# Attention outputs stored undivided, row sums inverted through DRAM

## The chip, the core and the metric

The kernel runs on one NeuronCore of a Trainium2 chip. TensorE (PE in the rows) multiplies matrices into PSUM, VectorE (DVE), ScalarE (ACT) and GpSimd (POOL) work on elements, and SyncE (SP) mostly issues DMAs; each of them takes its instructions strictly in order. The metric is the device time of one execution in microseconds (us). Two runs of the same kernel agree to a fraction of a per cent.

## The reference

A two-layer transformer backbone on 1024 latent and 256 context tokens of width 1024. Layer 0 mixes tokens by eight heads of latent attention (and, beside them, four heads of gated linear attention); layer 1 uses a gated delta rule; each layer ends in a squared-ReLU MLP. The change touches the attention heads of layer 0 and what reads their output:

```python
s = jnp.einsum('bhqd,bhkd->bhqk', qblk, k).astype(F32) * scale
p = jax.nn.softmax(s, axis=-1).astype(v.dtype)
return jnp.einsum('bhqk,bhkv->bhqv', p, v)
...
return jnp.concatenate([att, gla.reshape(B, L, GLA_HEADS * GLA_DV)], axis=-1) @ w_out
```

The softmax divides each query's exponentials by their sum, so an output may be accumulated undivided and divided later, by one number per head and query.

## The kernel before

Features lie on the partitions and tokens along the free dimension, in three blocks (`BLOCKS`): tokens 0 to 511, 512 to 1023, and the 256 context tokens. Every matrix product is made of three passes of reduced precision: each operand is split into a leading part (`...h`, `hi`, made by an ACT copy) and a rest (`...l`, `lo`, made by a subtraction on POOL or DVE), and PE adds hi·hi, hi·lo and lo·hi (lines 181 to 183).

**Attention** goes over heads 0 to 7, within a head over the three query blocks, and within a block over ten tiles of 128 keys (two for the context block): 176 steps. A step computes transposed scores `S` (three matmuls), takes their exponential `P` on ACT (L907), splits it into `ph` (ACT or DVE, L911 and L913) and `pl` (POOL, in one step of four DVE, L914), and four steps later multiplies it with the values (`pv`, lines 873 to 875). The value tile `Vh` carries 64 columns of ones, so PSUM tile `acc` holds 64 rows of outputs and 64 equal rows of the sums of the exponentials. At the last key tile of a block, 24 times in all, DVE inverts the 64 rows of sums (L878), multiplies (L880), and SP stores the result into `d_mix` in DRAM (L882). Beside this, `max_ops` finds the row maxima of the next blocks' scores (PE matmuls `M` L855, DVE reductions `mx` L856 and `mr` L858, PE `pr` L862), and `pair_ops` projects keys and queries of the next two heads.

**Output projection** (`out_proj`): `prep0(k, b)` loads chunk k of 128 features (two heads for k below 4) of block b from `d_mix` into `mx_in` (L806) and splits it. Block 0 is prepared while heads 6 and 7 still run; pass 0 multiplies it with the eight column blocks m of the weights, and meanwhile the 16 chunks of blocks 1 and 2 are prepared for pass 1. DVE also adds each result to the residual (`h`, L969) and adds up products for a modulation (`acc`, L124 and L126, fed by `adaw` DMAs on SP's queue); at the end of pass 0 PE sums squares (`st`, L252).

The Python code is a sequence of emissions. The build may place an instruction ahead of others that it doesn't depend on, so the order on an engine is read from the built program.

Of the kernel before, what the change touches and what calls it, by code (L numbers as in the profile page):

```python
# [33 lines left out]
def hybrid_backbone(ctx: ExitStack, tc: tile.TileContext, a, out, taps=None):  # L34
# [25 lines left out]
    def pump(us):  # L60
        """advances every lane: a lane yields the vector engine's time of what it emitted, or None to wait for the next call."""
        for it in list(lanes):
            gen, w = it
            t = us * w
            while t > 0:
                try:
                    d = next(gen)
                except StopIteration:
                    lanes.remove(it)
                    break  # L70
                if d is None:
                    break
                t -= d
# [39 lines left out]
    def ada_lane(l, mods, cols, wpool, accpool, ppool, ptag, wait=1):  # L113
        """modulations of layer l: products on the vector engine, sums over the partitions on the tensor engine."""
# [25 lines left out]
    def ada_first(m, half, wpool, ypool, ppool):  # L140
        """half of a modulation of layer 0 before there is other work: products on the tensor engine, then transposed."""
# [43 lines left out]
    def group(ps, n, nk, w, x, rate, every=1e9):  # L185
        """ps = sum over k of w(k)^T x(k), split operands; the lanes advance by rate of its time."""
# [12 lines left out]
    def rsqrt_small(p, ssq, n, dim, gain=1.0):  # L199
        """ssq: AP [128, n] (sums); returns tile [128, n] with gain/sqrt(mean + eps): a seed from the exponent, a step of  # L200
        third and one of second order."""
# [16 lines left out]
    def rsqrt_pool(p, ssq, n, dim):  # L218
        """as rsqrt_small, on the pool engine."""
# [13 lines left out]
    def stat_lane(hs, c0, n, tp, small, pp, ptag, dim, inc=False, engs=(V, G)):  # L233
        """1/rms of the tokens c0..c0+n over the features in the tiles hs, [128 tokens, n/128]; inc: as the tiles are made."""
# [22 lines left out]
    def spread(r, nt, pp, ptag):  # L257
        """r [128 tokens, nt] along the free dimension, the same on every partition: PSUM [128, nt * 128]."""
# [10 lines left out]
    def norm_lane(hs, c0, n, A, B, dst, tp, small, pp, ptag, r=None, inc=False, rb=None, ks=range(KD)):  # L269
        """a = rms(h) * A + B of a block of tokens, split into dst(k)."""  # L270
# [21 lines left out]
    class Act:  # L292
        """split activations [features, tokens] in tiles of one block of tokens."""
# [13 lines left out]
    # =========================================================== layer 0 mixer  # L307
# [8 lines left out]
    d_mix = [dram.tile([128, T], F32, name=f"d_mix{i}") for i in range(KD)]  # L316

# [13 lines left out]
    def gla_gates(g):  # L331
        """per head: decays of both directions (partitions 0..63 forward, 64..127 backward), decayed queries and keys."""
# [62 lines left out]
    def gla_main(g):  # L395
        """per head: states before every chunk, outputs, norm over the head, gate; transposed into d_mix."""
        f_order = list(range(16, 20)) + list(range(16))
        b_order = list(range(19, 15, -1)) + list(range(15, -1, -1))
        for h in range(4):
# [4 lines left out]
            # a chunk's outer product goes to the slot of the state after it  # L404
# [109 lines left out]
    with ExitStack() as e1:  # L514
# [146 lines left out]
        def latent(j, i, hs):  # L661
            """a chunk of the query (j = 0) or key-value (j = 1) latents, with its part of the sums of squares."""
# [26 lines left out]
    # ---- multi-head latent attention: scores transposed, minus the queries' maxima in a row of the contraction  # L689
# [7 lines left out]
    def proj(m, nm, kt, xh, xl, w, pp, tag):  # L697
        """generator of the projected blocks."""
# [8 lines left out]
    with ExitStack() as e2:  # L707
# [26 lines left out]
        # values  # L734
# [12 lines left out]
        # rotated query parts, scaled  # L747
# [46 lines left out]
    lp, wm = [None], [None]  # L794
# [7 lines left out]
    def prep0(k, b, eng):  # L802
        """a chunk of the heads' outputs, split for the output projection."""
        c0, n = BLOCKS[b]
        x = lp[0].tile([128, 512], F32, name="mx_in")
        nc.sync.dma_start(out=x[:, :n], in_=d_mix[k][:, c0:c0 + n])  # L806
        split(x[:, :n], *mix.at(k, c0, n), eng)

    with ExitStack() as e2:
# [8 lines left out]
        def pair_ops(m):  # L818
            """projections of the heads 2m, 2m + 1 into their slots, a block of tokens at a time."""
# [24 lines left out]
        def max_ops(hd, b):  # L844
            """the row maxima of the scores of a block of queries into the contraction's last row: subtracted as rounded to
            the leading part, which the softmax does not depend on."""
# [19 lines left out]
        def pv(st):  # L866
# [9 lines left out]
            if last:  # L876
                rt = op_.tile([64, 512], F32, name="rt")
                V.reciprocal(out=rt[:, :n], in_=o[64:128, :n])  # L878
                ot = op_.tile([64, 512], F32, name="ot")
                V.tensor_tensor(out=ot[:, :n], in0=o[0:64, :n], in1=rt[:, :n], op=ALU.mult)  # L880
                r0 = 64 * (hd % 2)
                nc.sync.dma_start(out=d_mix[hd // 2][r0:r0 + 64, c0:c0 + n], in_=ot[:, :n])  # L882

        acc = [None]
        steps = []
# [11 lines left out]
        for hd, b, j, last in steps:  # L897
# [27 lines left out]
            if (hd, b, j) == (7, 1, 9):  # L925
# [7 lines left out]
        for st in pend:  # L933
            pv(st)
    ea.close()
    elp.close()

    # =========================================================== output projection, residual; MLP
# [7 lines left out]
    def out_proj(l, wname, passes, mix, prep, base, act, add, stack, wp, w, span, sp=None):  # L946
        """h = base + gate * (mix @ w) in passes over blocks of tokens; prep[b]: what makes the blocks of pass b."""
# [42 lines left out]
    def mlp(l, blocks, tail_blocks, act, lanes_in, tail, wp, then=None):  # L990
        """h += gate * mlp(act); lanes_in(pools) makes the blocks after the first, tail(pools, b) follows a finished block."""
# [70 lines left out]
    with ExitStack() as e1:  # L1062
        mp = pool(e1, "mixT")
        mix.add(mp, "mx", BLOCKS[1:2])
        lp[0] = pool(e1, "lo", 3)
# [31 lines left out]
    # =========================================================== layer 1 mixer: gated delta rule  # L1097
# [720 lines left out]
```

## Time and profile before

| | us |
|---|---|
| timed runs | 3552.53, 3552.6, 3554.66 |
| median | 3552.6 |
| profiled execution: span from first to last instruction | 3550.4 |
| TensorE busy | 3322.8 (94%) |
| VectorE busy | 2329.7 (66%) |
| attention stage, from 575 to 933 us of the span | 358 |

No other time of the profiled execution is given than its span; it stands 2.2 us below the median of the timed runs, and that is taken for what lies around the span. In the rows below a busy TensorE isn't one at its peak, since matmuls overlap; how many matmuls start in a stretch tells more. "[2.60 <-DVE ot L880]" behind a row says that the engine was idle for 2.60 us before it, until that instruction ended. SPq is SP's queue of DMA issues. PEclk is the granted clock of TensorE as a share of 2.4 GHz.

### The profile page before, as it was taken

The page shows a single profiled execution, that of the slowest core. Times are in us where ns is not written, and L with a number is a line of the kernel's source. Part 1 is how long each engine was busy: PE and PEld are TensorE (multiplying, and loading weights), DVE is VectorE, ACT ScalarE, POOL GpSimd, SP SyncE. Part 2 cuts the span into 40 slices and gives each one's busy share as a digit, 9 for nine tenths or more (in the row PEclk, how much of TensorE's full clock was granted, in tenths as well). Part 3 has the DMA queues.
Part 4 walks back from the last instruction along what each step waited for, and adds up shares of the span by engine and source line. Part 5 has one row for each costly group of instructions (what it writes and reads, how often), then busy time and mean ns, then how long its engine had stood idle before and what let it go on. Part 6 is the DMA issues. An engine that isn't in the chain of part 4 may idle for free.

```text
span 3550.4 us, 47773 instructions
## 1 busy us (share of the span) xinstructions
PE 3322.8 (94%) x18372; PEld 2736.7 (77%) x18372; DVE 2329.7 (66%) x3986; ACT 1156.1 (33%) x2153; POOL 1077.5 (30%) x809
## 2 busy tenths in 40 slices
PE   8998988999989999999999997877999999999998
PEld 4876766666778888888888776666888788888887
DVE  4847556888768777776445779998466554444445
ACT  3143336555423111111211453332465421111212
POOL 3212125556642111111211332334025522222223
PEclk9988889999989999999999999998999999999999
DMA  5622224101422222221111233333664211111111
GB/s 191 216 71 64 59 92 105 26 21 50 149 88 84 75 82 80 76 82 62 45 39 36 72 101 90 90 83 103 143 131 131 72 48 48 48 48 48 48 54 60
DMA packets 279155, 285.06 MB, mean 80 GB/s; under 512 B 152176, under 2 KB 217264, under 8 KB 278928
## 3 DMA queue, kind: packets, MB, share of 16 engines
q1 hardware_dynamic: 267120, 260.78, 25.3%
q0 software_dynamic: 5760, 10.75, 1.3%
q10 hardware_dynamic: 6048, 10.49, 0.9%
q8 instruction: 144, 2.36, 0.3%
q14 instruction: 83, 0.68, 0.1%
HBM read 228.67 MB, written 53.28 MB: 79 GB/s over the span
## 4 chain that ended last, share of the span: by engine, by line
PE 71%; DVE 17%; issue 4%; ACT 3%; DMA 3%; POOL 2%; SPq 0%; DVEq 0%; ACTq 0%; POOLq 0%
PE ps L181 17%; PE ps L183 17%; PE ps L182 17%; DVE acc L126 2%; DVE tm L1371 2%; DVE gst L445 1%; DMA adaw<-in_adaw_dram 1%; DVE X L1373 1%; PE S L181 1%; DVE y L1151 1%; PE S L183 1%; PE S L182 1%; PE pa L1620 1%; DVE X L1365 1%; PE M L855 1%
## 5 line engine op out<-in xcount | busy, mean ns | idle before, releaser
L170 POOL TENSOR_TENSOR wlo<-wst,whi 128x1024 fp32r<-128x1024 f32 (+1 forms) x207 | 488.6, 2368 | 1553.1 <-ACT whi L167 1528.4
L181 PE MATMUL ps<-th,whi 128*128 128x512 f32 (+1 forms) x1304 | 480.5, 368 | 4.9 <-DVE h L1045 3.4
L183 PE MATMUL ps<-th,wlo 128*128 128x512 f32 (+1 forms) x1304 | 477.4, 366 | 2.4 <-POOL wlo L170 2.4
L167 ACT CAST whi<-wst 128x1024 fp32r<-128x1024 f32 (+2 forms) x213 | 212.6, 1012 | 820.1 <-PE ps L182 740.1
L182 PE MATMUL ps<-tl,whi 128*128 128x512 f32 (+1 forms) x1304 | 478.4, 367 | 0.0
L1010 DVE TENSOR_TENSOR rl<-rl 128x512 f32<-128x512 f32 (+1 forms) x160 | 214.5, 1341 | 346.0 <-ACT rl L1009 345.8
L181 PE MATMUL ps<-mxh,whi 128*128 128x512 f32 (+1 forms) x1008 | 356.5, 354 | 0.0
L183 PE MATMUL ps<-mxh,wlo 128*128 128x512 f32 (+1 forms) x1008 | 351.1, 349 | 1.1 <-POOL wlo L170 1.1
L182 PE MATMUL ps<-mxl,whi 128*128 128x512 f32 (+1 forms) x1008 | 351.5, 349 | 0.0
L126 DVE SCALAR_TENSOR_TENSOR acc<-adaw,sc,acc 128x256 f32<-128x256 f32 (+1 forms) x476 | 293.8, 661 | 42.5 <-DMA adaw<-in_adaw_dram 42.0
L1045 DVE SCALAR_TENSOR_TENSOR h<-ps,mod,h 128x512 f32<-128x512 f32 (+1 forms) x384 | 243.8, 657 | 96.4 <-PE ps L183 94.7
L181 PEld LDWEIGHTS ps<-th,whi 128*128 128x128 f32 x1304 | 247.4, 190 | 48.7 <-DVE h L1045 4.7
L183 PEld LDWEIGHTS ps<-th,wlo 128*128 128x128 f32 x1304 | 247.0, 189 | 43.6 <-POOL wlo L170 3.2
L182 PEld LDWEIGHTS ps<-tl,whi 128*128 128x128 f32 x1304 | 247.6, 190 | 38.9
L1045 DVE SCALAR_TENSOR_TENSOR g<-ps,mod,g 128x512 f32<-128x512 f32 (+1 forms) x264 | 188.5, 731 | 106.3 <-PE ps L183 106.1
L914 POOL TENSOR_TENSOR pl<-P,ph 128x512 fp32r<-128x512 f32 x144 | 179.7, 1262 | 114.3 <-DVE ph L913 78.9
L181 PEld LDWEIGHTS ps<-mxh,whi 128*128 128x128 f32 x1008 | 194.4, 193 | 25.8 <-issue 1.2
L182 PEld LDWEIGHTS ps<-mxl,whi 128*128 128x128 f32 x1008 | 194.4, 193 | 24.9 <-issue 1.4
L183 PEld LDWEIGHTS ps<-mxh,wlo 128*128 128x128 f32 x1008 | 194.2, 193 | 25.0 <-POOL wlo L170 1.5
L183 PE MATMUL ps<-m1h,wlo 128*128 128x512 f32 x512 | 203.9, 398 | 0.0
L181 PE MATMUL ps<-m1h,whi 128*128 128x512 f32 x512 | 203.8, 398 | 0.0
L182 PE MATMUL ps<-m1l,whi 128*128 128x512 f32 x512 | 203.6, 398 | 0.0
(373 smaller groups left out, 7011.6 us busy)
## 6 DMA issues: line engine op xcount, KB each, us to landing
wst<-in_w_dram SPq DMA_DIRECT2D x128, 512.0 KB, 3.5
adaw<-in_adaw_dram SPq DMA_DIRECT2D x224, 128.0 KB, 2.1
adaw<-in_adaw_dram SPq DMA_DIRECT2D x80, 256.0 KB, 3.6
wst<-in_owT_dram SPq DMA_DIRECT2D x25, 512.0 KB, 3.8
wst<-in_ewo_dram SPq DMA_DIRECT2D x16, 512.0 KB, 3.7
wY<-d_YA SPq DMA_DIRECT2D x64, 128.0 KB, 3.2
wst<-in_owo_dram SPq DMA_DIRECT2D x16, 512.0 KB, 3.7
wst<-in_ewT_dram SPq DMA_DIRECT2D x14, 512.0 KB, 4.6
```

The source lines that it names most:

```text
L126: V.scalar_tensor_tensor(out=acc[c], in0=w, scalar=sc[:, k, c:c + 1], in1=acc[c], op0=ALU.mult, op1=ALU.add)
L167: S.copy(out=hi, in_=src)
L170: lo_eng.tensor_tensor(out=lo, in0=src, in1=hi.bitcast(F32), op=ALU.subtract)
L181: PE.matmul(ps, hi_w, hi_x, start=first, stop=False)
L182: PE.matmul(ps, hi_w, lo_x, start=False, stop=False)
L183: PE.matmul(ps, lo_w, hi_x, start=False, stop=last)
L445: V.scalar_tensor_tensor(out=stt[p0:p0 + 64, c2, :], in0=stt[p0:p0 + 64, c, :], scalar=ge[p0:p0 + 64, c:c + 1], in1=stt[p0:p0 + 64, c2, :] ...
L855: PE.matmul(ps[:, :kn_], qh[0:96, qt * 128:(qt + 1) * 128], kh[0:96, k0:k0 + kn_], start=True, stop=True)
L914: (V if j % 4 == 3 else G).tensor_tensor(out=pl[:, :n], in0=P_[:, :n], in1=ph[:, :n].bitcast(F32), op=ALU.subtract)
L1010: V.tensor_tensor(out=r[:, :n], in0=r[:, :n], in1=r[:, :n], op=ALU.mult)
L1045: V.scalar_tensor_tensor(out=h[m][:, c0:c0 + n], in0=ps[:, :n], scalar=mod[l][:, 40 + m, c:c + 1], in1=h[m][:, c0:c0 + n], op0=ALU.mult, o ...
L1371: V.tensor_tensor(out=t3, in0=X[:, k + 1:, k:k + 1].to_broadcast([128, n, k]), in1=X[:, k:k + 1, :k].to_broadcast([128, n, k]), op=ALU.mult)
```

## The change

The division leaves the attention stage. At the last key tile ACT copies 65 rows of `acc` (64 of outputs, one of sums) into SBUF; SP stores the sums into `d_sum` and the undivided outputs into `d_mix`. After both heads of a pair have stored a block, `rcp_ops` loads their sums as 128 partitions by 8 (or 4) numbers, inverts these on DVE three steps later, and stores them into `d_rcp`. `prep0` loads the inverses for k below 4, each row repeated over 64 partitions, and DVE multiplies (`mx_r`, new line 813). In pass 1 the pool has two `mx_in` buffers and one `mx_r` where it had three `mx_in`. `prep0(3, 0)` is emitted later, at the last step. The rest of the diff takes out comments.

```diff
+    d_sum = dram.tile([8, T], F32, name="d_sum")
+    d_rcp = dram.tile([8, T], F32, name="d_rcp")
...
-    lp, wm = [None], [None]
+    lp, wm = [None, 2], [None]
...
         x = lp[0].tile([128, 512], F32, name="mx_in")
         nc.sync.dma_start(out=x[:, :n], in_=d_mix[k][:, c0:c0 + n])
+        if k < 4:
+            r = lp[0].tile([128, 512], F32, name="mx_r", bufs=lp[1])
+            for i in range(2):
+                nc.sync.dma_start(out=r[64 * i:64 * i + 64, :n], in_=d_rcp[2 * k + i, c0:c0 + n].partition_broadcast(64))
+            V.tensor_tensor(out=x[:, :n], in0=x[:, :n], in1=r[:, :n], op=ALU.mult)
         split(x[:, :n], *mix.at(k, c0, n), eng)
...
             if last:
-                rt = op_.tile([64, 512], F32, name="rt")
-                V.reciprocal(out=rt[:, :n], in_=o[64:128, :n])
-                ot = op_.tile([64, 512], F32, name="ot")
-                V.tensor_tensor(out=ot[:, :n], in0=o[0:64, :n], in1=rt[:, :n], op=ALU.mult)
+
+                ot = op_.tile([65, 512], F32, name="ot")
+                S.copy(out=ot[:, :n], in_=o[0:65, :n])
                 r0 = 64 * (hd % 2)
-                nc.sync.dma_start(out=d_mix[hd // 2][r0:r0 + 64, c0:c0 + n], in_=ot[:, :n])
+                nc.sync.dma_start(out=d_sum[hd:hd + 1, c0:c0 + n], in_=ot[64:65, :n])
+                nc.sync.dma_start(out=d_mix[hd // 2][r0:r0 + 64, c0:c0 + n], in_=ot[0:64, :n])
+                if hd % 2:
+                    rcps.append(rcp_ops(hd // 2, c0, n))
+
+        def rcp_ops(m, c0, n):
+
+            w = n // 64
+            sm = small.tile([128, 8], F32, name="sm")
+            for i in range(2):
+                nc.sync.dma_start(out=sm[64 * i:64 * i + 64, :w], in_=d_sum[2 * m + i, c0:c0 + n].rearrange("(q w) -> q w", w=w))
+            for _ in range(3):
+                yield
+            sq = small.tile([128, 8], F32, name="sq")
+            V.reciprocal(out=sq[:, :w], in_=sm[:, :w])
+            for i in range(2):
+                nc.sync.dma_start(out=d_rcp[2 * m + i, c0:c0 + n].rearrange("(q w) -> q w", w=w), in_=sq[64 * i:64 * i + 64, :w])
...
-            if (hd, b, j) == (7, 1, 9):
+            for x in list(rcps):
+                if next(x, 1):
+                    rcps.remove(x)
+            if (hd, b, j) == (7, 2, NT - 1):
                 prep0(3, 0, G)
...
+        for x in rcps:
+            run(x)
...
-        lp[0] = pool(e1, "lo", 3)
+        lp[:] = pool(e1, "lo", 2), 1
```

In the built program, first place: VectorE at the end of head 1 and the start of head 2. Before, from the inversion of block 1 of head 1 on:

```order
L878 RECIPROCAL rt<-acc 64x512
L913 CAST ph<-P 128x512
L880 TENSOR_TENSOR ot<-acc,rt 64x512
L856 TENSOR_REDUCE mx<-M 128x1 x2
L914 TENSOR_TENSOR pl<-P,ph 128x512
L856 TENSOR_REDUCE mx<-M 128x1 x2
L878 RECIPROCAL rt<-acc 64x256
```

Now, the same stretch, with the inversions of both heads' sums, blocks 1 and 2 (old L914, L856 and L913 are L937, L863 and L936):

```order
L937 TENSOR_TENSOR pl<-P,ph 128x512
L863 TENSOR_REDUCE mx<-M 128x1 x2
L936 CAST ph<-P 128x512
L902 RECIPROCAL sq<-sm 128x8
L863 TENSOR_REDUCE mx<-M 128x1 x2
L865 TENSOR_REDUCE mr<-mx 128x4
L936 CAST ph<-P 128x512
L902 RECIPROCAL sq<-sm 128x4
```

The long inversions and the products behind them have left the place; two inversions of 8 and 4 numbers per partition stand some rows later.

Second place: VectorE where attention ends and the projection begins. Before (`h_7919` is the first residual sum of pass 0):

```order
L878 RECIPROCAL rt<-acc 64x512
L878 RECIPROCAL rt<-acc 64x256
L880 TENSOR_TENSOR ot<-acc,rt 64x512
L880 TENSOR_TENSOR ot<-acc,rt 64x256
L124 TENSOR_SCALAR acc_8023<-adaw,sc 128x256
L124 TENSOR_SCALAR acc_8024<-adaw,sc 128x256
L126 SCALAR_TENSOR_TENSOR acc_8023<-adaw,sc,acc_8023 128x256
L126 SCALAR_TENSOR_TENSOR acc_8024<-adaw,sc,acc_8024 128x256
L969 SCALAR_TENSOR_TENSOR h_7919<-ps,mod_79,h_7919 128x512
```

Now (`h_7997` is that sum, line 813 the product for chunk 3 of block 0):

```order
L813 TENSOR_TENSOR mx_in<-mx_in,mx_r 128x512
L902 RECIPROCAL sq<-sm 128x8
L124 TENSOR_SCALAR acc_8101<-adaw,sc 128x256
L124 TENSOR_SCALAR acc_8102<-adaw,sc 128x256
L126 SCALAR_TENSOR_TENSOR acc_8101<-adaw,sc,acc_8101 128x256
L126 SCALAR_TENSOR_TENSOR acc_8102<-adaw,sc,acc_8102 128x256
L902 RECIPROCAL sq<-sm 128x4
L997 SCALAR_TENSOR_TENSOR h_7997<-ps,mod_79,h_7997 128x512
```

Ahead of the first residual sum VectorE now has a product and two inversions that depend on DMAs, where it had 6 us of its own work.

Third place: SP's queue there. Before, from the last store of an output to the first weights of the projection behind it:

```order
L882 DMA d_mix_104<-ot 64x256
L121 DMA adaw<-in_adaw_dram 128x256 x2
L806 DMA mx_in<-d_mix_104 128x512
L806 DMA mx_in<-d_mix_105 128x512
L121 DMA adaw<-in_adaw_dram 128x256
L806 DMA mx_in<-d_mix_106 128x512
L121 DMA adaw<-in_adaw_dram 128x256
L174 DMA wst<-in_ewo_dram 128x1024
```

Now, behind the same store:

```order
L898 DMA sm<-d_sum 64x8
L121 DMA adaw<-in_adaw_dram 128x256 x2
L898 DMA sm<-d_sum 64x4
L808 DMA mx_in<-d_mix_101 128x512
L904 DMA d_rcp<-sq 64x8 x2
L121 DMA adaw<-in_adaw_dram 128x256
L904 DMA d_rcp<-sq 64x4 x2
L121 DMA adaw<-in_adaw_dram 128x256
L812 DMA mx_r<-d_rcp 64x512 x2
L121 DMA adaw<-in_adaw_dram 128x256
L808 DMA mx_in<-d_mix_102 128x512
L121 DMA adaw<-in_adaw_dram 128x256
```

The loads of sums, the stores of inverses and the loads of `mx_r`, each of which waits for the one before, now stand among the loads for pass 1, with the `adaw` loads and the next weights behind them.

## Rows read from the trace of the kernel before

**Rows 1.** The page: its span, and TensorE's busy time over the span.
```profile
span 3550.4 us, 47773 instructions
PE 3322.8 (94%) x18372; PEld 2736.7 (77%) x18372; DVE 2329.7 (66%) x3986; ACT 1156.1 (33%) x2153; POOL 1077.5 (30%) x809
```
**Rows 2.** Windows: us; PE, PEld, DVE, ACT, POOL busy (count); PEclk, DMA, GB/s.
```profile
575.00:933.00 358.00, 331.71 (x1464) 251.95 (x1463) 292.82 (x420) 193.91 (x345) 223.92 (x194) 0.96 0.12 31
575.00:600.00 25.00, 23.83 (x94) 18.23 (x94) 15.66 (x30) 14.12 (x23) 13.90 (x12) 0.84 0.03 6
675.00:700.00 25.00, 21.77 (x91) 16.16 (x90) 19.08 (x27) 10.48 (x19) 11.19 (x10) 0.93 0.04 9
825.00:850.00 25.00, 20.50 (x75) 14.78 (x74) 20.23 (x23) 14.52 (x25) 24.27 (x17) 0.84 0.36 108
875.00:900.00 25.00, 25.00 (x119) 19.90 (x119) 20.30 (x29) 13.97 (x25) 16.55 (x14) 1.00 0.03 6
```
**Rows 3.** The tile rt: count, duration in ns (min/median/max), first and last start.
```profile
L878 DVE RECIPROCAL rt<-acc x24: 1689/3358/3360, 602.9 to 934.2; 64x512 f32<-64x512 f32 x16, 64x256 f32<-64x256 f32 x8
L880 DVE TENSOR_TENSOR ot<-acc,rt x24: 406/682/683, 606.6 to 936.5; 64x512 f32<-64x512 f32 x16, 64x256 f32<-64x256 f32 x8
```
**Rows 4.** Waits, 575 to 933 us: us in total, times, longest.
```profile
POOL pl L914 <- DVE ph L913: 78.9, 42, 8.8
...
PE pr L862 <- DVE mr L858: 8.1, 8, 2.6
PE acc L873 <- DVE ot L880: 7.2, 4, 2.6
```
**Rows 5.** Timeline around the end of head 1: start, duration.
```profile
665.82 3.36 DVE L878 RECIPROCAL rt<-acc 64x512 f32<-64x512 f32 x1
...
671.60 0.77 PE L873 MATMUL acc<-ph,Vh 128*128 128x512 f32 x1 [2.60 <-DVE ot L880]
```
**Rows 6.** Timeline, 676 to 690 us, in the same columns.
```profile
678.81 0.15 DVE L858 TENSOR_REDUCE mr<-mx 128x4 fp32r<-128x12 f32 x1
...
682.23 4.56 DVE L914 TENSOR_TENSOR pl<-P,ph 128x512 fp32r<-128x512 f32 x1
...
682.51 3.72 POOL L914 TENSOR_TENSOR pl<-P,ph 128x512 fp32r<-128x512 f32 x3
...
687.00 0.41 PE L862 MATMUL pr<-identr,mr 128*128 128x128 f32 x2 [2.65 <-DVE mr L858]
```
**Rows 7.** Exponentials, 575 to 933 us: busy us, mean ns, idle before.
```profile
L907 ACT ACTIVATE P<-S 128x512 f32<-128x512 f32 (+1 forms) x176 | 101.6, 578 | 134.8 <-PE S L183 130.4 <-POOL pl L914 3.5
```
**Rows 8.** The tile ot: its stores (issue in ns) and their landing.
```profile
L882 SPq DMA_DIRECT2D d_mix<-ot x24: 445/446/1384, 607.3 to 937.2; - x24
...
DMA to landing us min/median/max: 1.9/2.2/5.2
```
**Rows 9.** The tile mx_in: its issues, its splits, its landings.
```profile
L806 SPq DMA_DIRECT2D mx_in<-d_mix x24: 319/330/861, 547.9 to 970.8; - x24
...
L170 DVE TENSOR_TENSOR mxl<-mx_in,mxh x8: 416/682/2612, 939.6 to 976.0; 128x512 fp32r<-128x512 f32 x4, 128x256 fp32r<-128x256 f32 x4
...
DMA to landing us min/median/max: 2.0/3.5/5.7
```
**Rows 10.** Windows of pass 0 of the projection.
```profile
935.00:945.00 10.00, 10.00 (x46) 8.28 (x45) 8.30 (x14) 3.38 (x6) 4.59 (x2) 1.00 0.81 268
...
975.00:985.00 10.00, 4.74 (x21) 3.58 (x20) 9.08 (x11) 2.93 (x4) 5.91 (x4) 0.86 0.54 159
```
**Rows 11.** Waits, 935 to 1030 us.
```profile
PE st L252 <- DVE sq L243: 9.5, 1, 9.5
```
**Rows 12.** Timelines of VectorE and of GpSimd in pass 0.
```profile
930.92 4.97 DVE L878 RECIPROCAL rt<-acc 64x512 f32<-64x512 f32 x2 [1.75 <-PE acc L875]
...
976.60 4.23 DVE L126 SCALAR_TENSOR_TENSOR acc<-adaw,sc,acc 128x256 f32<-128x256 f32 x4 [0.21 <-DMA adaw<-in_adaw_dram]
...
977.36 2.39 POOL L170 TENSOR_TENSOR wlo<-wst,whi 128x1024 fp32r<-128x1024 f32 x1 [0.21 <-ACT whi L167]
```

More of the change, by code (lines that the diff above doesn't have):

```diff
@@ L876, in pv @@
             if last:
-                rt = op_.tile([64, 512], F32, name="rt")
-                V.reciprocal(out=rt[:, :n], in_=o[64:128, :n])
-                ot = op_.tile([64, 512], F32, name="ot")
-                V.tensor_tensor(out=ot[:, :n], in0=o[0:64, :n], in1=rt[:, :n], op=ALU.mult)
+                ot = op_.tile([65, 512], F32, name="ot")
+                S.copy(out=ot[:, :n], in_=o[0:65, :n])
                 r0 = 64 * (hd % 2)
-                nc.sync.dma_start(out=d_mix[hd // 2][r0:r0 + 64, c0:c0 + n], in_=ot[:, :n])
+                nc.sync.dma_start(out=d_sum[hd:hd + 1, c0:c0 + n], in_=ot[64:65, :n])
[13 more added lines that the diff above has]
+                nc.sync.dma_start(out=d_rcp[2 * m + i, c0:c0 + n].rearrange("(q w) -> q w", w=w), in_=sq[64 * i:64 * i + 64, :w])
         acc = [None]
+        rcps = []
         steps = []
```

## Prediction

> **What bounds the kernel now.** I read the page first, then windows of the attention stage, then the waits in it, and last two timelines. The page has TensorE busy for 94% of a span of 3550.4 us [rows 1], so only time that TensorE loses can be won. Busy time hides part of that loss, since matmuls overlap; the reader should look at how many start. In a window without loss 119 start in 25 us, 4.76 per us, at full clock [rows 2]. Over the 358 us of the stage 1464 start, which at that rate take 307.6 us. So TensorE loses about 50 us there (shorter matmuls are mixed in everywhere, so this is an estimate to some us). VectorE is busy for 292.8 of the 358 us, 82%, the fullest engine after TensorE.
>
> The waits say how the two are joined: POOL waited 78.9 us for `ph` from VectorE, and TensorE itself 7.2 us for the product `ot` in 4 waits and 8.1 us for `mr` in 8 [rows 4]. The timeline shows one such piece: an inversion of 3.36 us starts at 665.82, what is queued behind it on VectorE comes late, and TensorE stands for 2.60 us until `ot` has left the PSUM tile that the next block needs [rows 5]. The granted clock then falls to a mean of 0.93 in the window from 675 to 700 [rows 2], which is a stretch at the lower of its two levels, 1.2 GHz.
>
> **What goes.** From VectorE go 24 inversions (16 of 3.36 us and 8 of 1.69 us: 67.3 us) and 24 products (16 of 0.68, 8 of 0.41: 14.2 us) [rows 3], 81.5 us in all, 6 of them behind the last matmul of attention. Its share in the stage falls from 82% to about 61%, with the 4 us that come in (below).
>
> Not all of TensorE's 50 us is theirs. The window from 575 to 600 lies ahead of the first inversion at 602.9 [rows 3]; its 94 matmuls need 19.7 us, so 5.3 us are lost to the start. The window from 825 to 850 starts 75, worth 15.8 us, and loses 9.2; POOL is busy for 24.27 us of it [rows 2] with splitting weights, so I leave it half, 4.6. That leaves 40.5 us. Directly shown as waits for VectorE are 7.2 + 8.1 = 15.3 us [rows 4]; the mean clock of 0.96 is worth 0.04 × 358 = 14.3 us, of which the two windows just named hold 0.16 × 25 = 4.0 each [rows 2], so 6.3 follow stalls elsewhere. These 21.6 us I count in full. Of the other 18.9 us, small waits that no row names, I count a third, 6.3, because one cause of late VectorE work stays: at 682.23 a subtraction with two SBUF inputs took 4.56 us while POOL ran three of its own for 3.72 us, and TensorE then waited 2.65 us for `mr` [rows 6]. Gain: 28 us. The bounds are 10 (the waits for `ot` and half of the clock's 6.3) and 40.5.
>
> **What comes into the attention stage.** 24 copies go to ACT, at 0.58 us like its exponentials from PSUM [rows 7], some 13 us on an engine that is busy for 193.9 of 358 us [rows 2] and waits for `S` most of the rest; hidden, since outputs are taken up four steps after their scores; uncovered, each would push one exponential by 0.6 us. Twelve small inversions cost little by themselves: the nearest small operation takes 0.15 us [rows 6], and eight numbers at the pace of a long inversion (3.36 us for 512) another 0.05; 12 × 0.2 = 2.4 us. But each stands in VectorE's order behind two DMAs in series, a store of 0.45 us issue and 2.2 us landing and a load like it [rows 8]: about 6 us from the copy on, against about three steps, 4.5 to 5.6 us. VectorE may stand 1 us each time, and four products for block 0 also wait for loads. Queued behind are `mx`, `ph` and `pl`; VectorE has 39% of the stage free for it. SP's queue has nothing else urgent there. Cost to TensorE: 3 us, between 0 and 12.
>
> **The projection's first chunk 3.** TensorE takes up chunk 3 of block 0 about 70 matmuls behind the last one of head 7, block 0: 14.7 us at 4.76 per us. The new path is a copy 0.6, store 0.45 + 2.2, load 0.45 + 2.2, inversion 0.2, two stores 0.9 + 2.2, two loads 0.7 + 3.5, product 0.7, split 0.6 + 1.3: 16.0 us [rows 8, 9 and 7]. TensorE stands 2 us; with landings at their maxima of 5.2 and 5.7 [rows 8, 9] it would be 13, with shorter ones 0.
>
> **Pass 0.** Here VectorE is already what TensorE waits for: it is busy for 9.08 of 10 us from 975 on, TensorE for 4.74 [rows 10], and TensorE stands 9.5 us for the sum of squares [rows 11]. Three things change. First, two inversions of 4.97 us and products of 1 us, up to 936.9, go [rows 12], about 4 us behind the end of attention; in their place VectorE's first residual sum stands behind an inversion at the end of a copy, two DMAs and their issues: 0.6 + 2 × 0.45 + 2 × 2.2 to 2 × 5.2 + 0.2, so 6 to 12 us behind the end; DMA is 0.81 busy [rows 10], so I take 8, and VectorE starts 4 us later. Second, eight products of two SBUF tiles come; the nearest row is the split by VectorE, 0.42 to 2.61 us, median 0.68 [rows 9]. Six stand ahead of the sum of squares; at 1.0 each, 6 us. Third, VectorE idles 1.7 us of the 10 at 935 and 0.9 at 975 [rows 10], so about 5 us in the 40 between, of which I let 3 be filled. Cost: 4 + 6 − 3 = 7 us. The bounds are −4 (all but the inversions that go is hidden) and 25.
>
> On the products the trace has this: an `acc` group of four that shares 2.39 us with POOL's weight split takes 4.23 us [rows 12], and the same split on VectorE ranges from 0.42 to 2.61 us [rows 9]. The Trainium skill, SBUF — State Buffer, section "Who interferes with whom", says that a Vector instruction with two SBUF inputs and a GpSimd instruction that reads SBUF exclude each other, and that whichever comes second waits until the first is through. By that rule the products that go, which read one operand from PSUM, never met POOL, and the eight that come can; the rows of `acc` agree. What it would come to is worked out from rows as rival (d).
>
> **The sum.** −28 + 3 + 2 + 7 = −16 us. The span goes from 3550.4 to 3534.4; with the 2.2 us by which it stands below the median of the timed runs, 3536.6: about 3537 us. Its own range is 3520 to 3545.
>
> **Rivals.**
> (a) The long inversions made nearly all of the loss and the tail is hidden: −40.5 + 3 = −37.5, 3515 us. For it: VectorE falls to 61%. Against it: rows 6 show a wait that POOL made.
> (b) TensorE's losses stay, made by POOL's hold on VectorE and by the chain from scores to `pl`: only the 10 us of the lower bound go, and the 12 that come (3 + 2 + 7) eat them: +2, 3555 us, no change. For it: POOL idles for `ph` more than for anything, and TensorE is 94% busy.
> (c) Slower, by one mechanism: in pass 0 the single `mx_r` buffer and SP's order put each product behind a load that is issued when the product before it has ended, 0.7 of issue and 3.5 of landing, and the `adaw` loads and weights behind that. VectorE stands for it when the work between two products is shorter than 4.2 us plus what SP has ahead. Four such waits whole, 17 us, with products at 2.61 (six: 16) and the start's 4, make 37 against the gain of 28 less 5: +14, 3567 us. It decides once pass 0 loses over 23 us. Against it: the built program leaves five or more VectorE operations between any two of the first four products.
> (d) Each of the six products that stand ahead of the sum of squares is held by a whole weight split: 6 × (0.68 + 2.39) = 18 us where I count 6 [rows 9, 12]. The sum is then −16 + 12 = −4: 3549 us. For it: the group of four in rows 12. Against it: the median of the split on VectorE is 0.68, so most of them met nothing. This is the page's rule at its full weight.
>
> Chances: forecast 0.51, (a) 0.15, (b) 0.14, (d) 0.07, (c) 0.13. Under 0.2%, 7 us, no change can be told here; so faster 0.66 (forecast and (a)), within 0.2% 0.21 ((b) and (d)), slower 0.13. The range that leaves out some 2 in 10 reaches into (a) and over (b) and (d) to the near part of (c): 3512 to 3562 us.
>
> **What would show it.** In the profile after: attention shorter by some 25 us from its first score to its last output; VectorE near 61% there; no wait of TensorE for `ot` over 1 us; waits for `mr` fewer, but not none. Windows of pass 0 with VectorE still fullest and the wait for the sum of squares at 15 to 20 us instead of 9.5; a wait of about 2 us for chunk 3. It is wrong if the wait for the sum of squares stays under 10 us (then (a)), if attention is less than 12 us shorter (then (b)), or if that wait passes 30 us (then (c)).

## The result and the profile after

The changed kernel takes 3523.07 us in the median of four runs (3521.12 to 3529.43) where the kernel before, on the same chip, takes 3553.63. The ratio is 0.991, with a 95% interval of 0.9896 to 0.9924, so 27 to 37 us less. Forecast were 3537 us and 16 us less: the sign and the range are right, the gain was put too low. The measured time lies 14 us below the forecast and 8 above the 3515 of rival (a).

The page after gives the span and the busy times, as [rows 1] do for before:

```profile
span 3527.7 us, 47903 instructions
PE 3316.6 (94%) x18372; PEld 2738.6 (78%) x18372; DVE 2240.6 (64%) x3962; ACT 1170.1 (33%) x2177; POOL 1079.3 (31%) x809
```

VectorE has 89 us less to do, TensorE the same work within 7 us. This profiled run is the slowest of the four (3529.43), so stages are compared below by their length, not by the span.

How long attention lasts is read from its 176 exponentials, whose first and last start stand in the rows of tile `P`. Columns: count, duration in ns (min/median/max), first and last start in us. Before and after:

```profile
L907 ACT ACTIVATE P<-S x176: 383/597/602, 577.5 to 928.8; 128x512 f32<-128x512 f32 x160, 128x256 f32<-128x256 f32 x16
```

```profile
L930 ACT ACTIVATE P<-S x176: 377/598/603, 582.5 to 902.1; 128x512 f32<-128x512 f32 x160, 128x256 f32<-128x256 f32 x16
```

From first to last it was 351.3 us and is 319.6: 31.7 us are won here. The starts of the two differ by 5 us for no reason of the change (574.3 to 590.7 in the profiles of this study), which is why stages are compared by their length.

Windows of the stage and of 100 us in its middle, after (columns as in [rows 2]):

```profile
575.00:902.00 327.00, 316.93 (x1457) 248.55 (x1458) 218.25 (x397) 205.32 (x365) 222.98 (x196) 0.97 0.15 37
700.00:800.00 100.00, 99.71 (x480) 79.66 (x479) 70.09 (x131) 65.61 (x119) 65.60 (x62) 1.00 0.12 27
```

In the middle 480 matmuls start in 100 us at full clock, against 476 at the rate without loss (4.76 per us): TensorE loses nothing there any more. Over the stage 1457 starts need 306.1 us, so about 21 of 327 us are lost, where it was 50 of 358. VectorE is busy for 67% instead of 82%.

What TensorE waited for between 600 and 800 us, before and then after (us in total, times, longest):

```profile
PE pr L862 <- DVE mr L858: 7.0, 6, 2.6
PE acc L873 <- DVE ot L880: 5.2, 2, 2.6
PE acc L875 <- POOL pl L914: 1.2, 2, 0.6
```

```profile
PE pr L869 <- DVE mr L865: 0.5, 2, 0.3
```

The wait for `ot` of [rows 5] is gone, and in this stretch so is the wait of 2.65 us for `mr` of [rows 6], which the prediction had put down to GpSimd. Over the whole stage waits for `mr` remain, 6.4 us where [rows 4] have 8.1; all but 0.5 us of them lie before 600 and behind 800 us (us in total, times, longest, 575 to 903 us after):

```profile
PE pr L869 <- DVE mr L865: 6.4, 6, 2.3
```

What came in, after: the copies and the small inversions (same columns as tile `P`; the second line is VectorE's wait for the loads of the sums, us and times).

```profile
L886 ACT COPY ot<-acc x24: 357/580/583, 606.0 to 905.1; 65x512 f32<-65x512 f32 x16, 65x256 f32<-65x256 f32 x8
```

```profile
L902 DVE RECIPROCAL sq<-sm x12: 165/188/203, 655.8 to 914.4; 128x8 f32<-128x8 f32 x8, 128x4 f32<-128x4 f32 x4
...
  DMA sm<-d_sum: 8.8, 3
```

Of the 8.8 us 5.9 lie behind the last matmul of attention; in the stage itself the chain cost VectorE 2.9 us of idle time.

Pass 0 is read from the last exponential to the first matmul that sums squares (`st`, [rows 11]). Before it was 928.8 to 989.22, 60.4 us. After, the window between attention and `st`, and waits in it:

```profile
905.00:968.00 63.00, 47.15 (x202) 38.62 (x201) 39.28 (x55) 16.88 (x25) 28.64 (x15) 0.88 0.77 231
```

```profile
PE st L252 <- DVE sq L243: 10.0, 1, 10.0
DVE acc L126 <- DMA adaw<-in_adaw_dram: 9.6, 6, 3.3
...
PE adat L133 <- DVE acc L126: 5.8, 1, 5.8
DVE mx_in L813 <- issue: 4.9, 2, 2.7
...
DVE mx_in L813 <- DMA mx_r<-d_rcp: 2.8, 1, 2.8
```

TensorE still stands for the sum of squares as in [rows 11], and for 5.8 us more at a new place: `adat`, which waits for an `acc` whose `adaw` came late. From 902.1 to 967.82 it is 65.7 us, 5.3 more than before. VectorE is no longer the full engine there: 39.28 of 63 us, where it was 48.76 of 57. The timeline of SP shows where the `adaw` loads stand (start, duration):

```profile
923.78 1.09 SPq L812 DMA_DIRECT2D mx_r<-d_rcp  x2
926.50 0.33 SPq L808 DMA_DIRECT2D mx_in<-d_mix  x1
926.87 1.36 SPq L121 DMA_DIRECT2D adaw<-in_adaw_dram  x2
930.30 0.33 SPq L174 DMA_DIRECT2D wst<-in_ewo_dram  x1
931.50 1.09 SPq L812 DMA_DIRECT2D mx_r<-d_rcp  x2
```

Loads for the division, of the next chunk, of `adaw` and of weights take turns, and there are gaps between SP's issues.

### The profile page after: what moved, and what is told of

Read it like the earlier page. It is cut to its first block, busy times and chain, and to the rows that moved or that the text cites. A ratio compares the mean times of both kernels' runs of the same rounds, so it can differ in the third digit from the quotient of the medians.

```text
span 3527.7 us, 47903 instructions
## 1 busy us (share of the span) xinstructions
PE 3316.6 (94%) x18372; PEld 2738.6 (78%) x18372; DVE 2240.6 (64%) x3962; ACT 1170.1 (33%) x2177; POOL 1079.3 (31%) x809
## 4 chain that ended last, share of the span: by engine, by line
PE 72%; DVE 17%; issue 4%; ACT 3%; DMA 3%; POOL 2%; SPq 0%; DVEq 0%; ACTq 0%; POOLq 0%
PE ps L181 17%; PE ps L182 17%; PE ps L183 17%; DMA adaw<-in_adaw_dram 2%; DVE acc L126 2%; DVE tm L1399 2%; PE S L181 1%; PE S L182 1%; PE S L183 1%; DVE X L1401 1%; DVE y L1179 1%; DVE gst L447 1%; PE pa L1648 1%; PE acc L880 1%; PE acc L882 1%
## 5 line engine op out<-in xcount | busy, mean ns | idle before, releaser
L183 PE MATMUL ps<-mxh,wlo 128*128 128x512 f32 (+1 forms) x1008 | 351.3, 349 | 0.0
L126 DVE SCALAR_TENSOR_TENSOR acc<-adaw,sc,acc 128x256 f32<-128x256 f32 (+1 forms) x476 | 286.7, 645 | 49.1 <-DMA adaw<-in_adaw_dram 48.8
L937 POOL TENSOR_TENSOR pl<-P,ph 128x512 fp32r<-128x512 f32 x144 | 178.8, 1249 | 87.9 <-DVE ph L936 57.7
```

Of the source, the lines that this page charges most:

```text
L126: V.scalar_tensor_tensor(out=acc[c], in0=w, scalar=sc[:, k, c:c + 1], in1=acc[c], op0=ALU.mult, op1=ALU.add)
L183: PE.matmul(ps, lo_w, hi_x, start=False, stop=last)
L937: (V if j % 4 == 3 else G).tensor_tensor(out=pl[:, :n], in0=P_[:, :n], in1=ph[:, :n].bitcast(F32), op=ALU.subtract)
```

## The experiments

All were timed in five rounds against the kernel before on the same chip. Runs scatter more on these chips than on the first (the kernel before: 3544 to 3567 us), and the intervals reach 5 to 9 us to either side. The kernel before has a median of 3552 to 3555 us there, so rows are compared by their ratios. In the two profiles of the changed kernel attention, measured as above, agrees to 0.5 us and pass 0 to 2.2. "Attention" and "pass 0" in the table are these two lengths.

| kernel | attention | pass 0 | median us | ratio to before (95%) |
|---|---|---|---|---|
| before | 351.3 | 60.4 | | |
| changed, first profile | 319.6 | 65.7 | 3523.07 | 0.9910 (0.9896 to 0.9924) |
| changed, again | 320.1 | 68.0 | 3523.27 | 0.9908 (0.9889 to 0.9927) |
| no division | 318.1 | 61.0 | 3524.52 | 0.9914 (0.9891 to 0.9936) |
| copies on VectorE | 319.7 | 65.5 | 3522.58 | 0.9906 (0.9886 to 0.9926) |
| before, copy for inversion | 320.9 | 59.8 | 3524.91 | 0.9908 (0.9884 to 0.9932) |
| changed + 24 long inversions | 351.0 | 69.3 | 3562.0 | 1.0029 (1.0015 to 1.0043) |
| the same in halves | 326.7 | 65.0 | 3535.95 | 0.9954 (0.9938 to 0.9969) |
| the same in quarters | 319.4 | 66.5 | 3526.48 | 0.9926 (0.9900 to 0.9952) |
| before, inversion in quarters | 331.3 | 63.5 | 3537.79 | 0.9959 (0.9943 to 0.9975) |
| that, product on GpSimd | 334.5 | 64.0 | 3540.14 | 0.9959 (0.9945 to 0.9973) |
| `mx_r` loads from GpSimd | 319.9 | 74.1 | 3534.26 | 0.9943 (0.9928 to 0.9958) |
| products without loads | 320.0 | 63.7 | 3523.28 | 0.9909 (0.9891 to 0.9927) |
| chunks 0 to 2 divided early | 321.8 | 65.3 | 3529.98 | 0.9935 (0.9917 to 0.9954) |

**The changed kernel again.**

> The changed kernel once more, unchanged, with a second profile. Theory: attention ends about 31 us earlier than before in every execution (last output near 906 us instead of 937), and pass 0 of the projection gives some of it back, in the first profile through a wait of 6.0 us of TensorE for the sum of an acc group (adat) that was short of adaw loads; the give-back varies with the DMAs, so the second profile shows between 0 and 6 us there, and the time is 3520 to 3530 us. Rival: the 6.0 us wait is a property of the program's order and comes again at the same size, with the same span of 3528 within 2 us in the profile.

The stages came again (320.1 and 68.0 us). The wait for `adat`, 8.8 us, is above the theory's 0 to 6 and is not the rival's 6.0 either, though the span, 3527.4, is the rival's: the wait belongs to the program, and its size varies.

**No division.**

```diff
-                nc.sync.dma_start(out=d_sum[hd:hd + 1, c0:c0 + n], in_=ot[64:65, :n])
-                if hd % 2:
-                    rcps.append(rcp_ops(hd // 2, c0, n))
-        if k < 4:
-            r = lp[0].tile([128, 512], F32, name="mx_r", bufs=lp[1])
...
-            V.tensor_tensor(out=x[:, :n], in0=x[:, :n], in1=r[:, :n], op=ALU.mult)
```

> The changed kernel without the stores of sums, the small inversions and the loads and products with inverses (the division is left out). Theory: what stands in pass 0 for the division costs about 7 to 10 us there, and none in attention; so 7 to 10 us below the changed kernel, near 3514 us, with attention ending at the same time within 2 us, no wait for adat of over 3 us and a wait for the sum of squares that is not longer. Rival: pass 0 waits for VectorE and DMA anyway, and the division hides in it: within 3 us of the changed kernel.

In the stages the signs of the theory come: pass 0 at 61.0 us, no wait for `adat`, attention 1.5 to 2 us shorter. The size is 4.7 and 7.0 us in pass 0, under or at the low end of its 7 to 10. The time is the rival's: the two ratios cover each other, with intervals of 7 and 8 us to either side.

**Copies on VectorE.**

```diff
-                S.copy(out=ot[:, :n], in_=o[0:65, :n])
+                V.tensor_copy(out=ot[:, :n], in_=o[0:65, :n])
```

> The changed kernel with the 24 copies of the outputs on VectorE instead of ScalarE. Theory (VectorE's total time in attention is what delays TensorE): the copies bring back about 14 us (16 of 0.68, 8 of 0.41) of the 81.5 us that left VectorE, so about 14/81.5 of the 31 us of attention, 5 us: near 3528 us. Rival (it is the engine that frees the PSUM tile acc: on VectorE the copy queues behind other work, and TensorE waits for it): waits of TensorE for ot come back, over 5 us in sum, and the time rises by 10 us or more.

Neither: attention takes 319.7 us, so 14 us of short work on VectorE cost nothing, and no wait for `ot` came back. ScalarE is not what made the gain.

**The kernel before with a copy where it inverts.**

```diff
-                V.reciprocal(out=rt[:, :n], in_=o[64:128, :n])
+                V.tensor_copy(out=rt[:, :n], in_=o[64:128, :n])
```

> The kernel before with a copy of the sums (0.68 and 0.41 us) where it inverts them (3.36 and 1.69 us), so the division is left out; its products, stores and the whole projection stay as they were. VectorE has 53 us less in attention, and TensorE still waits for the product that frees acc. Theory: 20 to 28 us of attention go, nothing is given back in pass 0: 3525 to 3533 us. Rival (it is the place of the release on ScalarE that counts, not VectorE's time): under 10 us go, over 3543 us.

More than the theory's 20 to 28 us: shortening the inversions alone gives 30.4 of the 31.7 us, with VectorE still freeing `acc`, and pass 0 stays as it was.

**24 long inversions put back, and the same work in pieces.** A hold is here the time for which one instruction keeps VectorE. The first is this; in the others the columns of `ot` are put on a list, and the loop over steps takes one piece from it per step (four quarters, or two halves).

```diff
                 S.copy(out=ot[:, :n], in_=o[0:65, :n])
+                V.reciprocal(out=one64[:, :n], in_=ot[0:64, :n])
...
+        one64 = op_.tile([64, 512], F32, name="one64", bufs=1)
```

> The changed kernel with 24 more inversions on VectorE, 64x512 or 64x256 from the copied output in SBUF into a tile that nobody reads, at the old places behind each block's last product; the PSUM tile acc is still freed by ScalarE's copy. From the first to the last exponential attention took 351.3 us before, 319.6 and 320.0 in two profiles of the changed kernel. Theory 1 (one long instruction holds back what is queued behind it on VectorE): it goes back by 15 us or more, to 335 to 351 us, and the time to 3538 to 3552 us. Theory 2 (VectorE's total load): the same here. Theory 3 (TensorE waited for the release of acc by VectorE): under 326 us, near 3525 us.

> As the run with 24 long extra inversions, but each cut into four pieces of a quarter of the columns (128 or 64, about 0.85 or 0.45 us), one in each of the next four steps: the same work on VectorE in all, and no long hold. Theory 1 (the long hold): attention stays under 326 us from first to last exponential, near 3525 us. Theory 2 (total load): over 335 us, as with the long ones, over 3538 us. Theory 3 (release of acc): under 326 us.

This pair decides. The extra inversions, long and in quarters (the pieces of the last two blocks are left out in quarters and halves; columns as for tile `P`):

```profile
L887 DVE RECIPROCAL one<-ot x24: 1731/3337/3345, 615.2 to 947.9; 64x512 f32<-64x512 f32 x16, 64x256 f32<-64x256 f32 x8
```

```profile
L953 DVE RECIPROCAL one<-ot x88: 525/933/945, 614.5 to 904.4; 64x128 f32<-64x128 f32 x60, 64x64 f32<-64x64 f32 x28
```

Windows of the same 100 us, long and in quarters:

```profile
700.00:800.00 100.00, 92.41 (x413) 70.88 (x412) 81.12 (x121) 55.07 (x101) 60.59 (x55) 0.95 0.11 24
```

```profile
700.00:800.00 100.00, 99.62 (x476) 79.28 (x474) 83.85 (x152) 64.98 (x119) 67.75 (x65) 1.00 0.12 27
```

VectorE is busier in quarters (83.85 against 81.12 us) and TensorE loses nothing; in long pieces it starts 413 matmuls instead of 476. The 63 missing starts are worth 13 us, of which the granted clock, 0.95 against 1.00, is about 5. Attention goes back to 351.0 us, the length before to 0.3 us, though ScalarE frees `acc` and nobody reads the result. So it is the hold, not VectorE's load and not the release of `acc`. One rival is left: the whole ones stand right behind the block's copy, the pieces at another place in the step, and whole ones at that place were not run. Halves and quarters do stand at the same place (below). The time with the long ones, 3562 us, is above the 3538 to 3552 expected, and 0.15% to 0.43% above before, 5 to 15 us; this fits attention as before and the changed kernel's pass 0, 8.9 us longer in this profile.

What stands between a hold and TensorE is seen in the run with the long ones (timeline, start and duration; then TensorE's waits from 600 to 800 us):

```profile
685.22 1.73 DVE L887 RECIPROCAL one<-ot 64x256 f32<-64x256 f32 x1
...
686.88 0.35 DVE L938 CAST ph<-P 128x512 fp32r<-128x512 f32 x1
...
687.38 1.27 POOL L939 TENSOR_TENSOR pl<-P,ph 128x512 fp32r<-128x512 f32 x1 [2.15 <-DVE ph L938]
...
691.87 0.53 POOL L844 DMA_DIRECT2D Ql<-d_pel  x1 [1.75 <-PE S L183]
...
692.21 4.49 DVE L939 TENSOR_TENSOR pl<-P,ph 128x512 fp32r<-128x512 f32 x1
...
692.42 3.73 POOL L939 TENSOR_TENSOR pl<-P,ph 128x512 fp32r<-128x512 f32 x3
...
696.63 0.41 DVE L863 TENSOR_REDUCE mx<-M 128x1 f32<-128x256 f32 x1
697.07 0.15 DVE L865 TENSOR_REDUCE mr<-mx 128x2 fp32r<-128x2 f32 x1
...
697.38 0.66 PE L869 MATMUL pr<-identr,mr 128*128 128x128 f32 x2 [2.87 <-DVE mr L865]
```

```profile
PE pr L869 <- DVE mr L865: 9.0, 7, 2.9
PE acc L882 <- POOL pl L939: 3.7, 4, 1.1
```

This is the picture of [rows 6] again: GpSimd has three subtractions to catch up with, VectorE's own is held beside them, and `mr` is late. GpSimd's backlog has two parts in these rows: it stood 2.15 us for a `ph` that ran right behind an inversion of 1.73 us, and 1.75 us at its own issue of the load of `Ql` (queries of the next heads), until a matmul of `S` had ended. Before, it stood 1.93 us at that issue (681.97) ahead of the subtraction of [rows 6]; the changed kernel has no such wait in this stage. It is not enough by itself: with halves GpSimd stands there for 2.83 and 2.80 us, and no subtraction on VectorE takes longer than 2.71. VectorE's 32 subtractions of `pl`, before, after, with long inversions and in quarters:

```profile
L914 DVE TENSOR_TENSOR pl<-P,ph x32: 623/681/4561, 584.5 to 924.4; 128x512 fp32r<-128x512 f32 x32
```

```profile
L937 DVE TENSOR_TENSOR pl<-P,ph x32: 674/692/2575, 588.6 to 898.4; 128x512 fp32r<-128x512 f32 x32
```

```profile
L939 DVE TENSOR_TENSOR pl<-P,ph x32: 628/938/4493, 597.0 to 937.1; 128x512 fp32r<-128x512 f32 x32
```

```profile
L940 DVE TENSOR_TENSOR pl<-P,ph x32: 617/682/2931, 596.3 to 905.8; 128x512 fp32r<-128x512 f32 x32
```

The subtractions of 4.5 us beside GpSimd come with the long inversions and go with them; there are two of them in the stage, before and with the long ones, so they account for some of TensorE's waits and not for the whole loss.

> The run with extra inversions, each cut into two halves (256 or 128 columns, about 1.75 or 0.93 us) in two consecutive steps. Whole ones (3.34 us) took attention to 351.0 us from first to last exponential, quarters (0.93 us) left it at 319.4. Theory A (cost in proportion to what a hold exceeds a quarter): (1.75 - 0.93) / (3.34 - 0.93) of 31.6 us, 11 us, so about 330 us and 3534 us. Theory B (a hold of up to a step, 320 us / 176 = 1.8 us, is absorbed whole): under 322 us, 3527 us. Theory C (every hold over a product's length costs): over 340 us, over 3545 us.

By the stage between A and B: pieces of 1.73 us take attention to 326.7 us, 7 us more than quarters, where proportion asked for 11; by the time, 3535.95 us, A. At the same place in a step, then, longer pieces cost more. That the cost grows faster than the length of the hold is not shown: there is one profile of each, and the whole ones stand elsewhere.

**The division kept in attention, in quarters.** From a copy of `acc`, with the product and the store in the fifth step; and the same with the product on GpSimd.

```diff
-                V.reciprocal(out=rt[:, :n], in_=o[64:128, :n])
+                S.copy(out=ot[:, :n], in_=o[:, :n])
+                divs.append(div_ops(hd, c0, n, ot))
+        def div_ops(hd, c0, n, ot):
+            for q in range(0, n, n // 4):
+                V.reciprocal(out=rt[:, q:q + n // 4], in_=ot[64:128, q:q + n // 4])
+                yield
+            V.tensor_tensor(out=ot[0:64, :n], in0=ot[0:64, :n], in1=rt[:, :n], op=ALU.mult)
```

> The kernel before with the division kept in attention, but from a copy of acc that ScalarE makes, the inversion cut into four pieces, one a step, the product and the store in the fifth; nothing of the division in the projection. Theory 1 (long hold): attention 320 to 326 us from first to last exponential, pass 0 (last exponential to the sum of squares) at 60 us as before where the changed kernel had 65.8 and 68.0: 3515 to 3525 us. Theory 2 (total load): attention over 335 us and no faster than 3538 us.

> The run with the division kept in attention and the inversion in four pieces, with its product on GpSimd instead of VectorE. That run took 331.2 us from first to last exponential where the changed kernel with the same extra pieces and no product took 319.4. Theory (the 24 products on VectorE, which then is busy for 87%, made these 12 us): 319 to 324 us, near 3528 us. Rival (the pieces' inverses were held by the copy, or GpSimd's subtractions of pl, which come late, are what counts): 328 us or more, 3535 us or more.

In both the theory of the long hold missed. Attention takes 331.3 us, between the two theories of the first, and 334.5, the second's rival, so the product's engine is not the cause of the 12 us between this and the extra quarters. Pass 0 is no longer 60 us either; the last divisions stand ahead of it, and TensorE waits for `adat` here too, 4.7 and 3.1 us, with no load of an inverse. What holds attention back I can't say: VectorE is at 87.5 us of 100 with the product and 86.3 without, against 83.9 in quarters. GpSimd waits longer for scores (17.8 and 16.2 us in the stage, 1.2 in the changed kernel), which may be a consequence. So short pieces alone do not make VectorE's work free.

**Loads of the inverses from GpSimd's queue.**

```diff
-                nc.sync.dma_start(out=r[64 * i:64 * i + 64, :n], in_=d_rcp[2 * k + i, c0:c0 + n].partition_broadcast(64))
+                (G if b else nc.sync).dma_start(out=r[64 * i:64 * i + 64, :n], in_=d_rcp[2 * k + i, c0:c0 + n].partition_broadcast(64))
```

> The changed kernel with the loads of the inverses for blocks 1 and 2 issued from GpSimd's queue instead of SP's. Theory (in pass 0 SP stands behind those loads, each of which waits for the product before it, and the adaw loads come late): the wait of TensorE for adat, 6.0 and 9.0 us in two profiles, falls under 3 us, and from the last exponential to the sum of squares it takes 60 to 63 us instead of 65.8 and 68.0; the time falls by 4 to 6 us. Rival (the products' own time on VectorE, or GpSimd's queue that now stands in turn with the weight splits behind it, makes the delay): 65 us or more, and the time is the same or higher.

Pass 0 and time are the rival's, 74.1 us and slower. Half of the theory came: VectorE waits 2.9 us for `adaw` (last line) instead of 9.6, and TensorE 3.5 for `adat`, as it would if the loads of the inverses on SP's queue held back `adaw`. But GpSimd now stands for the product before (12.1 us in 4 waits, first line), the weight split behind it comes late for TensorE, and TensorE waits 12.8 us for the sum of squares:

```profile
POOL mx_r L812 <- DVE mx_in L813: 12.1, 4, 3.6
POOL mx_r L812 <- DMA d_rcp<-sq: 10.3, 1, 10.3
...
PEld ps L183 <- POOL wlo L170: 5.7, 1, 5.7
...
DVE acc L126 <- DMA adaw<-in_adaw_dram: 2.9, 3, 1.3
```

**Products without loads.**

```diff
+            else:
+                V.tensor_tensor(out=r[:, :n], in0=x[:, :n], in1=x[:, :n], op=ALU.mult)
```

> The changed kernel with the loads of the inverses for blocks 1 and 2 left out; in their place VectorE squares the undivided chunk into the mx_r tile, a product of two SBUF inputs at the same eight places (the division of blocks 1 and 2 is left out). From the last exponential to the sum of squares it took 60.4 us before, 61.0 without any division, 65.5 to 69.2 in five profiles with the changed kernel's pass 0. Theory (the chain of loads on SP's queue makes the delay): 60 to 62 us, no wait of TensorE for adat over 2 us. Rival (the products' own time and GpSimd's hold on VectorE): 65 us or more.

In between, 63.7 us, with waits for `adat` of 6.3 us in 2 and a shorter one for `st` (3.1). So these loads are not the only cause of the wait for `adat`. The products, the start and the loads may share the 5 to 9 us; the runs do not part them.

**Chunks 0 to 2 divided early.**

```diff
-        if k < 4:
+        if k == 3:
...
+            x, r = (op_.tile([128, 512], F32, name=t, bufs=1) for t in ("xd", "rd"))
...
+            for _ in range(3):
+                yield
+            V.tensor_tensor(out=x[:, :n], in0=x[:, :n], in1=r[:, :n], op=ALU.mult)
+            nc.sync.dma_start(out=d_mix[m][:, c0:c0 + n], in_=x[:, :n])
```

> The changed kernel, but chunks 0 to 2 are divided while attention still runs: five steps after an inversion the undivided chunk and its inverses are loaded, multiplied on VectorE and stored back; the projection divides chunk 3 alone, so pass 0 has two products instead of eight. Theory (short work on VectorE is free in attention, the chain costs in pass 0): attention 319 to 323 us from first to last exponential, pass 0 at 61 to 64 us, 3 to 6 us below the changed kernel in the profile, at 3514 to 3523 us. Rival (what counts in pass 0 is the chain of the last head alone, which stays): pass 0 at 65 us or more, and the same time as the changed kernel.

The rival: pass 0 at 65.3 us with two products instead of eight, inside the 65.0 to 69.3 of the six profiles with the changed kernel's pass 0. That speaks for the last head's chain and the loads behind it as most of the cost, and does not show it. No kernel here is shown to be faster than the changed one.

## Why the prediction was right, and by how much it was off

- **The gain in attention (forecast 28).** Without any division the stage takes 318.1 us, 33.2 less than before: 33.2 of the 40.5 us that were the upper bound. The direction, the place and the engine were right. Too small was the step "Of the other 18.9 us, small waits that no row names, I count a third". Of the waits that were counted in full 8.9 us went in the changed kernel (7.2 for `ot`, 1.7 of 8.1 for `mr`), and the mean clock of 0.97 over 327 us leaves 9.8 us where it was 14.3, 4.5 less. By this estimate, good to some us, 18 of the 31.7 us won were small losses: nearly all of the 18.9 and not a third. The reason given, "one cause of late VectorE work stays", fell in its example: the 4.56 us subtraction beside GpSimd and the wait of 2.65 us for `mr` [rows 6] went with the inversions, are missing in quarters and came back with long ones. (That they come and go together is shown; each step from an inversion to GpSimd's backlog is not.) As a statement it held in part, since 6.4 us of waits for `mr` are left.
- **What comes into attention (3).** 1.5 to 2 us in the stages (319.6 and 320.1 against 318.1), VectorE's idle time for sums 2.9. The copies on ScalarE are hidden, and on VectorE they would be too.
- **Chunk 3 (2).** TensorE waited 0.3 us for a split of a chunk, nothing else.
- **Pass 0 (7).** 5.3 and 7.6 us in two profiles of the changed kernel, 4.6 to 8.9 in four more kernels that have its pass 0. Counted from the projection's first matmul it is 62.9 us where it was 56.0. The sum was right, its parts were not, and that they added up to the 7 is luck. The first residual sum starts 9.5 us behind the projection's first matmul (914.44 to 904.9) where it was 5.7 (938.91 to 933.2): 3.8 later, as the 4 said. But VectorE did not fill its idle time and did not stay the fullest engine. It stood for `adaw` (9.6 us, 5.1 before) and for the products' turn, and the five products that ran before the sum of squares took 4.2 us, with 7.7 us of idle time ahead of three of them.
- **The signs.** No wait for `ot`, fewer for `mr`, attention shorter by over 25 us: they came. "VectorE near 61% there" was worked out with the old length (218.25 of 358 us is 61%); of the shorter stage it is 67%. "15 to 20 us instead of 9.5" for the sum of squares did not (10.0 and 9.3); with the new wait for `adat` in front of it the two make 15.8 and 18.1. "If the wait for the sum of squares stays under 10 us (then (a))" was a bad sign, since the delay could come out at another instruction; 9.3 would have pointed at (a), with pass 0 7.6 us longer.
- **The rivals.** (a) was nearer than the forecast in the time (3515 and 3537 us, measured 3523), right that most of the loss was the inversions', though 33.2 and not 40.5, and wrong on the tail, which was not hidden. (b) is excluded by the result: attention is 31.7 us shorter. (c) began as described, SP behind the products, and stopped far short of 23 us. (d) did not come: the longest of the twelve products took 1.78 us, so none waited for a whole weight split of 2.39.
- **What stays open.** The gain was put 14 to 15 us too low. The terms above account for about 9 of it (5 in the hold, 1 in what comes in, 2 in chunk 3, 2 at most in pass 0). The stages give 31.7 less 5.3 or 31.2 less 7.6, 24 to 26 us, and the timed runs 27 to 37. For the copy in place of the inversion stages and time agree (31 and 30.5). With one profile of the kernel before, and a start of attention that varies by 16 us, these few us stay unexplained. So do the 12 to 15 us by which the division in quarters is longer in attention.

On the pair of rows at 692 us the Trainium skill, SBUF — State Buffer, section "Who interferes with whom", says that a VectorE instruction with two SBUF inputs and a GpSimd one that reads SBUF exclude each other. The trace agrees that the two meet (4.49 us, where the median in the changed kernel is 0.69), and it adds that VectorE stood through three of GpSimd's instructions in a row, though its own row starts 0.2 us ahead of theirs (692.21 and 692.42).

## What to carry to other kernels

The busy share of a helper engine does not say by itself what it costs: in the middle of the stage VectorE was busy for 81% with the long inversions put back, which cost some 32 us, and for 84% with the same work cut up, which cost nothing. Look at the longest instruction ahead of what TensorE waits for, and cut it or shrink it; then measure again, since with the division in quarters, at 86 to 88%, 12 to 15 us were lost though no piece was long. Before a wait is put down to another engine, ask what made that engine late; here the backlog on GpSimd came and went with the long inversions. Work that moves through DRAM may be paid where it is loaded again: pass 0 became 5 to 9 us longer, and loads that wait for one another, on the queue that also issues `adaw`, may be part of it.

## What the runs showed of the hardware

- A VectorE inversion of 64 rows takes 3.34 us for 512 columns from SBUF and 3.36 from PSUM, 1.73 and 1.69 for 256, and 128 columns take 0.93 to 0.95 us: cutting one into four costs about 0.4 us in all.
- The same inversions cost by the length of a piece and not by their sum: 16 of 3.34 us and 8 of 1.73 made attention 31.6 us longer than quarters did, pieces of up to 1.73 us 7, pieces of up to 0.95 us nothing against the changed kernel.
- A product of 64x512 from SBUF takes 1.29 us on GpSimd and 0.68 on VectorE.
